# A hybrid encoder layer on one core: one softmax minimum for both key halves, and division by the sums after the value products

## The chip, the cores and the metric

One core of one Trainium2 chip. The metric is device time in microseconds, of one launch of the whole kernel. TensorE does the matrix products, VectorE and ScalarE read and empty PSUM, GpSimd works on SBUF only, and all transfers are issued by SyncE (SP).

## What is computed

The reference is one encoder layer, run on a prompt of 1024 tokens ("p") and a sample of 512 tokens ("s"). Each goes through one input projection, then two groups of heads side by side (a gated delta rule, 8 heads, and dense latent attention, 8 heads), gates, one output projection and a norm. The change touches only the dense attention:

```python
s = jnp.einsum('bhqd,bhkd->bhqk', qi, k) * MLA_SCALE
p = jax.nn.softmax(s, axis=-1)
return jnp.einsum('bhqk,bhkd->bhqd', p, v)
...
mix = jnp.concatenate([o_a * jax.nn.silu(z_a), o_b * jax.nn.silu(z_b)], axis=-1)
```

## The kernel before

Products are made in float32 by splitting an operand into a rounded high part and the rest, and adding three products. The program has stages: the input projection of p, that of s beside the delta rule of p, the preparation of the attention, the attention of p beside the delta rule of s, the attention of s beside the first output projection, and the rest of the output projection.

TensorE's order is written out by hand in all of them: `merge` keeps a clock `self.t`, advanced by `cost` for each product (line 116), and takes the next piece from the first stream whose due time has come; if none is due, the clock jumps. The clock fixes the order alone: TensorE then runs that order as fast as its operands come. The delta rule's streams stand first (so they win when due), the attention next, the output projection last (it fills). The other engines are ordered by the framework.

In `attention` (line 943) a head's queries go in blocks of 256, a block in two tiles of 128 queries, a tile against its keys in pieces of 512: two halves for p (nh = 2, 64 tiles), one for s (nh = 1, 32 tiles).

- `scores` (line 1007): for each half five products into one of two PSUM banks "s" (lines 1030 to 1034), their minimum on VectorE (`am`, 1037; the scores carry a minus sign), the exponential on ScalarE with that half's own minimum and the row sum beside it (`pe`, `al`, 1038). After the second half: the common minimum (1046), exp of the difference (`af`, ScalarE, 1047), the corrected sum (1048), its reciprocal (1049) and the two factors (1050), all on columns of 1 or 2 elements; then GpSimd multiplies both halves of `pe` by their factor (1052). For s there is a reciprocal (1043) and one such product.
- `values` (line 1076): one step takes 256 keys of a block: four transposes of `pe` into the one PSUM bank `pt` (1091), the split of it into `pth` (ScalarE, 196) and `ptl` (VectorE, 199), and, for the step before, six products with the values into `po` (`pv`, 1060). A block of p needs four steps, one of s two. After the last, VectorE multiplies `po` by the gate `z` (tile `az`, two buffers, 1073) and SP writes it to the scratch tensor `mix` (1074), which the output projection reads later.
- `beside` (line 1105) sets the rhythm: one half of scores, one step of values, and so on. A half is due SLAT = 3.0 after the half before the last one ended, a step PLAT = 2.0 after the last step ended. A block's transposes begin LAG = 2 halves after it was queued.

In `run`, `attentions` (line 1311) runs p, then s after a delay, and `first` (line 1289) begins the output projection once the delta rule is done; its weights are split on ScalarE and GpSimd (`whi`, `wlo`, `piece`, line 201).

Of the kernel before, what the change touches and what calls it, by code (L numbers as in the profile page):

```python
# [7 lines left out]
F32 = mybir.dt.float32  # L8
# [3 lines left out]
AF = mybir.ActivationFunctionType  # L12
ALU = mybir.AluOpType
AX = mybir.AxisListType
# [3 lines left out]
P = 128  # L18
D = 2048
KT = D // P  # L20
H = 8
# [4 lines left out]
BLK = 512  # L26
# [2 lines left out]
GAP = 8  # L29
PLAT = 2.0  # L30
SLAT = 3.0


QKV0, ZA0, CQ0, CKV0, ZB0, LAST = 0, 24, 32, 36, 38, 46
# [23 lines left out]
class Kern:  # L58
# [884 lines left out]
    def attention(self, q, T, cp, ap, pss, ps1):  # L943
        nc, a, sm, S = self.nc, self.a, self.sm, self.scratch
        nt, nh = T // P, T // BLK
        QB = 256
        def twice(out, src):
            nc.sync.dma_start(out[:64], src)
            nc.sync.dma_start(out[64:], src)
# [17 lines left out]
                    nc.vector.tensor_sub(krl[:64, ks], r[:64], krs[:64, ks].bitcast(F32))  # L967
        for h in range(H):
            self.dt(f"mix{8 + h}{q}", [P, T])

        bank = lambda name: pss.tile([P, BLK], F32, tag="s", name=name, bufs=2)

# [34 lines left out]
        def scores(h, kh, kl, t0, pes):  # L1007
            tq = slice(t0, t0 + QB)
            qn = ap.tile([P, QB], F32, tag="qn", name="qn")
            qp = ap.tile([P, QB], F32, tag="qp", name="qp")  # L1010
            nc.sync.dma_start(qn, S[f"q{h}{q}"][:, tq])
            twice(qp, S[f"qr{h // 2}{q}"][h % 2 * 64:h % 2 * 64 + 64, tq])
            qh = ap.tile([P, QB], F32R, tag="qh", name="qh", bufs=2)
            ql = ap.tile([P, QB], F32R, tag="ql", name="ql", bufs=2)
            self.split(qh, ql, qn)

            qr = ap.tile([P, QB], F32R, tag="qr", name="qr", bufs=2)
            nc.scalar.activation(qr, qp, AF.Copy)
            nc.vector.tensor_sub(qr[64:], qp[64:], qr[64:].bitcast(F32))
            for i in range(QB // P):  # L1020
                qs = slice(i * P, (i + 1) * P)
                pe = []
                m = sm.tile([P, nh], F32, tag="am", name="am", bufs=4)
                l = sm.tile([P, nh], F32, tag="al", name="al", bufs=4)
                f = sm.tile([P, nh], F32, tag="af", name="af", bufs=4)
                for k in range(nh):
                    ks = slice(k * BLK, (k + 1) * BLK)
                    pe.append(ap.tile([P, BLK], F32, tag="pe", name="pe", bufs=8 if nh > 1 else 6))
                    o = bank("s")
                    nc.tensor.matmul(o, qh[:, qs], kh[:, ks], start=True, stop=False)  # L1030
                    nc.tensor.matmul(o, qh[:, qs], kl[:, ks], start=False, stop=False)
                    nc.tensor.matmul(o, ql[:, qs], kh[:, ks], start=False, stop=False)
                    nc.tensor.matmul(o, qr[:, qs], krs[:, ks], start=False, stop=False)
                    nc.tensor.matmul(o, qr[:, qs], krl[:, ks], start=False, stop=True)
                    self.cost(BLK, 5)

                    nc.vector.tensor_reduce(m[:, k:k + 1], o, axis=AX.X, op=ALU.min)  # L1037
                    nc.scalar.activation(pe[k], o, AF.Exp, bias=m[:, k:k + 1], scale=-1.0,  # L1038
                                         accum_out=l[:, k:k + 1])
                    if k == nh - 1:  # L1040
                        mm = sm.tile([P, 1], F32, tag="amm", name="amm", bufs=4)
                        if nh == 1:
                            nc.vector.reciprocal(f, l)
                        else:

                            nc.vector.tensor_tensor(mm, m[:, 0:1], m[:, 1:2], op=ALU.min)
                            nc.scalar.activation(f, m, AF.Exp, bias=mm, scale=-1.0)
                            nc.vector.scalar_tensor_tensor(l, l, 1.0, f, op0=ALU.mult, op1=ALU.mult, accum_out=mm)
                            nc.vector.reciprocal(mm, mm)
                            nc.vector.tensor_scalar(f, f, mm, None, op0=ALU.mult)  # L1050
                        for k2 in range(nh):
                            nc.gpsimd.tensor_mul(pe[k2], pe[k2], f[:, k2:k2 + 1].to_broadcast([P, BLK]))  # L1052
                    yield
                pes.append(pe)


        past, done, tick = [0.0, 0.0], [0.0], [0]
        queue, now, last = [], [None], [None]

        def pv(b, kb, hi, lo):  # L1060
            vh, vl = b["vs"]
            if kb == 0:
                b["po"] = ps1.tile([P, QB], F32, tag="po", name="po")
                b["z"] = ap.tile([P, QB], F32, tag="az", name="az", bufs=2)
                nc.sync.dma_start(b["z"], S[f"f{ZB0 + b['h']}{q}"][:, b["tq"]])
            po, z = b["po"], b["z"]
            for j in range(2):
                nc.tensor.matmul(po, vh[:, kb + j], hi[:, j], start=kb + j == 0, stop=False)
                nc.tensor.matmul(po, vh[:, kb + j], lo[:, j], start=False, stop=False)
                nc.tensor.matmul(po, vl[:, kb + j], hi[:, j], start=False, stop=kb + j == nt - 1)  # L1070
            self.cost(2 * QB, 3)
            if kb + 2 == nt:
                nc.vector.tensor_mul(z, po, z)
                nc.sync.dma_start(S[f"mix{8 + b['h']}{q}"][:, b["tq"]], z)

        def values():

            if now[0] is None and queue and queue[0]["tick"] <= tick[0]:
                now[0] = queue.pop(0)
                now[0]["kb"] = 0  # L1080
            b, new = now[0], None
            if b is None and last[0] is None:
                return
            yield max(self.t, done[0] + PLAT)
            if b is not None:
                kb = b["kb"]
                pt = ps1.tile([P, 2, QB], F32, tag="pt", name="pt")
                for j in range(2):
                    k, c = (kb + j) // 4, (kb + j) % 4 * P
                    for i in range(QB // P):  # L1090
                        nc.tensor.transpose(pt[:, j, i * P:(i + 1) * P], b["pes"][i][k][:, c:c + P], self.ident)  # L1091
                self.cost(2 * QB, 2)
                hi = ap.tile([P, 2, QB], F32R, tag="pth", name="pth", bufs=2)
                lo = ap.tile([P, 2, QB], F32R, tag="ptl", name="ptl", bufs=2)
                self.split(hi, lo, pt)
                new = b, kb, hi, lo
                b["kb"] += 2
                if b["kb"] == nt:
                    now[0] = None
            if last[0] is not None:  # L1100
                pv(*last[0])
            last[0] = new
            done[0] = self.t

        def beside(gen):
            while True:
                yield max(self.t, past[0] + SLAT)
                try:
                    next(gen)
                except StopIteration as e:  # L1110
                    return e.value
                past[:] = past[1], self.t
                tick[0] += 1
                yield from values()

        def finish():
            while queue or now[0] is not None or last[0] is not None:
                tick[0] += 1
                yield from values()

        vs = []
        for h in range(H):
            if h % 2 == 0:
                wk = self.piece(a["w_uk"][h // 2], nc.gpsimd, ap, "2", 2, rb=3 - nh)
            kh, kl = yield from beside(keys(h % 2, wk))
            for t0 in range(0, T, QB):
                pes = []
                yield from beside(scores(h, kh, kl, t0, pes))
                if h % 2 == 0 and t0 == 0:
                    yield from finish()  # L1130
                    wv = self.piece(a["w_uv"][h // 2], nc.gpsimd, ap, "2", 2, rb=3 - nh)
                    yield from beside(pair_values(wv, vs))
                queue.append({"h": h, "tq": slice(t0, t0 + QB), "pes": pes, "tick": tick[0] + LAG,
                              "vs": [v[:, :, h % 2 * P:(h % 2 + 1) * P] for v in vs]})
        yield from finish()


# [273 lines left out]
```

## Time and profile before

| | |
|---|---|
| median of 3 runs | 3258.99 us (3256.91 to 3262.88) |
| the profiled execution's own time | 3260.19 us |
| its span in the trace | 3258.2 us |
| busy: TensorE, VectorE, ScalarE, GpSimd | 96%, 51%, 36%, 28% |
| scores of p and s on TensorE | 2081.6 to 2760.0 us of the span |

The profiled execution is taken on its own time, which is 1.2 us above the median. Times in the rows are microseconds from the start of the span. A matmul's record lasts from its start to its modelled end, so that records overlap: what a product costs TensorE is the distance from its start to the next start.

### The profile page before, as it was taken

What the parts mean: (1) busy time and instruction counts of PE and PEld (TensorE: products, weight loads), DVE (VectorE), ACT (ScalarE), POOL (GpSimd) and SP (SyncE); (2) the same over time, 40 slices, a digit from 0 to 9 for tenths busy, and PEclk for the clock granted to TensorE, in tenths of its full rate; (3) what the DMA queues carried; (4) which work ended last, traced back from release to release, by engine and by line L of the source; (5) the groups of instructions that cost most, each with busy time, mean ns of one, the idle gap of its engine ahead of it and who ended that gap; (6) DMA issues with size and microseconds to landing.
All of it is one profiled execution on the core that took longest, in us unless ns stands there. A gap on an engine that the chain in (4) does not pass through costs nothing.

```text
span 3258.2 us, 47587 instructions
## 1 busy us (share of the span) xinstructions
PE 3137.4 (96%) x16554; PEld 2617.6 (80%) x16554; DVE 1655.6 (51%) x4000; ACT 1173.7 (36%) x2768; POOL 904.4 (28%) x838
## 2 busy tenths in 40 slices
PE   7999999999999899999999999899999999999998
PEld 6888888888888788888888777688787878777876
DVE  7233343444411636764675488788887555240213
ACT  4222222222211323333333243466666555432231
POOL 5322222222222300000000034222233444464452
PEclk9999999999999999999999999999999999999999
DMA  7555555555555765655655775432223242563554
GB/s 244 172 164 171 168 167 172 174 172 162 172 181 155 265 197 183 189 190 185 226 172 176 226 253 173 132 95 85 62 79 109 69 138 81 168 197 122 151 171 132
DMA packets 352624, 529.57 MB, mean 163 GB/s; under 512 B 84656, under 2 KB 135848, under 8 KB 350848
## 3 DMA queue, kind: packets, MB, share of 16 engines
q1 hardware_dynamic: 352384, 526.54, 51.6%
q8 instruction: 130, 2.13, 0.3%
q14 instruction: 110, 0.90, 0.1%
HBM read 336.01 MB, written 186.86 MB: 160 GB/s over the span
## 4 chain that ended last, share of the span: by engine, by line
PE 74%; DVE 10%; DMA 8%; issue 3%; ACT 2%; POOL 2%; SPq 1%; POOLq 0%; DVEq 0%; ACTq 0%
PE mm L241 15%; PE mm L245 15%; PE mm L242 15%; DMA wraw<-w_out 3%; PE py L1169 3%; PE py L1168 3%; PE py L1170 3%; PE pt L1091 2%; PE Tp L808 2%; POOL wlo L199 2%; DVE UA L703 1%; PE Fp L790 1%; PE py L871 1%; PE pu L890 1%; DVE tm L754 1%
## 5 line engine op out<-in xcount | busy, mean ns | idle before, releaser
L241 PE MATMUL mm<-hi,whi 128*128 128x512 f32 x2256 | 900.8, 402 | 13.8 <-DVE lo L272 7.3
L199 POOL TENSOR_TENSOR wlo<-wraw,whi 128x512 fp32r<-128x512 f32 x432 | 582.6, 1354 | 1091.7 <-ACT whi L196 926.3
L242 PE MATMUL mm<-lo,whi 128*128 128x512 f32 x2256 | 877.9, 391 | 6.6 <-DVE lo L272 6.6
L245 PE MATMUL mm<-hi,wlo 128*128 128x512 f32 x2256 | 763.8, 391 | 0.0
L196 ACT ACTIVATE whi<-wraw 128x512 fp32r<-128x512 f32 x432 | 270.1, 630 | 941.3 <-PE mm L242 597.0
L241 PEld LDWEIGHTS mm<-hi,whi 128*128 128x128 f32 x2256 | 425.9, 189 | 99.2 <-ACT whi L196 8.5
L242 PEld LDWEIGHTS mm<-lo,whi 128*128 128x128 f32 x2256 | 425.6, 189 | 91.1 <-DVE lo L272 9.4
L245 PEld LDWEIGHTS mm<-hi,wlo 128*128 128x128 f32 x2256 | 424.8, 188 | 91.2 <-DMA wlo<-wl43.4_7823 0.3
L1168 PE MATMUL py<-whi,mhi 128*128 128x512 f32 x768 | 303.5, 395 | 9.1 <-DVE y L1183 6.2
L1169 PE MATMUL py<-wlo,mhi 128*128 128x512 f32 x768 | 304.1, 396 | 6.8 <-POOL wlo L199 6.8
L1170 PE MATMUL py<-whi,mlo 128*128 128x512 f32 x768 | 302.6, 394 | 0.0
L1052 POOL TENSOR_TENSOR pe<-pe,af 128x512 f32<-128x512 f32 x160 | 166.3, 1057 | 372.5 <-DVE af L1050 197.4
L323 DVE SCALAR_TENSOR_TENSOR acc<-cin,conv_w,acc 128x1024 f32<-128x1024 f32 (+1 forms) x192 | 208.9, 1088 | 33.8 <-ACT acc L321 29.2
L319 DVE TENSOR_TENSOR cin<-mm,rbh 128x512 f32<-128x512 f32 x72 | 47.5, 688 | 318.8 <-PE mm L245 269.3
L1169 PEld LDWEIGHTS py<-wlo,mhi 128*128 128x128 f32 x768 | 145.0, 189 | 44.2 <-POOL wlo L199 12.8
L1168 PEld LDWEIGHTS py<-whi,mhi 128*128 128x128 f32 x768 | 145.0, 189 | 43.7 <-DVE y L1183 7.8
L1170 PEld LDWEIGHTS py<-whi,mlo 128*128 128x128 f32 x768 | 145.0, 189 | 32.1
L327 DVE TENSOR_TENSOR acc<-mm,rbh 128x512 f32<-128x512 f32 x48 | 31.7, 687 | 233.5 <-PE mm L245 233.3
L1183 DVE TENSOR_TENSOR y<-py,g 128x512 f32<-128x512 f32 x36 | 24.7, 690 | 240.3 <-ACT junk L1182 236.7
L1038 ACT ACTIVATE pe<-s,am 128x512 f32<-128x512 f32 x160 | 110.2, 689 | 89.4 <-DVE am L1037 79.0
L199 DVE TENSOR_TENSOR ptl<-pt,pth 128x512 fp32r<-128x512 f32 x160 | 110.0, 687 | 51.7 <-ACT pth L196 50.8
L329 ACT ACTIVATE ct<-acc 128x1024 f32<-128x1024 f32 (+1 forms) x80 | 68.2, 853 | 159.7 <-DVE acc L323 126.1
(449 smaller groups left out, 5106.6 us busy)
## 6 DMA issues: line engine op xcount, KB each, us to landing
wraw<-w_out SPq DMA_DIRECT2D x192, 256.0 KB
wraw<-w_in SPq DMA_DIRECT2D x188, 256.0 KB
dd<-dX SPq DMA_DIRECT2D x48, 256.0 KB
wraw<-w_uq SPq DMA_DIRECT2D x36, 256.0 KB
x<-xT_p SPq DMA_DIRECT2D x16, 512.0 KB
xres<-x_p SPq DMA_DIRECT2D x8, 1024.0 KB
y_p<-y SPq DMA_DIRECT2D x32, 256.0 KB
x<-xT_s SPq DMA_DIRECT2D x16, 256.0 KB
```

Of the source, the lines that this page charges most:

```text
L196: nc.scalar.activation(hi, src, AF.Copy)
L199: (lo_eng or nc.vector).tensor_sub(lo, src, hi.bitcast(F32))
L241: nc.tensor.matmul(ps, whi[:, k], hi[:, s], start=kt == 0, stop=False)
L242: nc.tensor.matmul(ps, whi[:, k], lo[:, s], start=False, stop=False)
L245: nc.tensor.matmul(ps, wlo[:, k], hi[:, s], start=False, stop=kt == KT - 1)
L323: nc.vector.scalar_tensor_tensor(acc, cin[:, j:j + T], w[:, f, j:j + 1], acc, op0=ALU.mult, op1=ALU.add)
L329: nc.scalar.activation(t, acc, AF.Tanh)
L1038: nc.scalar.activation(pe[k], o, AF.Exp, bias=m[:, k:k + 1], scale=-1.0, accum_out=l[:, k:k + 1])
L1052: nc.gpsimd.tensor_mul(pe[k2], pe[k2], f[:, k2:k2 + 1].to_broadcast([P, BLK]))
L1168: nc.tensor.matmul(ps, hi[:, c], w[0], start=kt == kts[0], stop=False)
L1169: nc.tensor.matmul(ps, hi[:, c], w[1], start=False, stop=False)
L1170: nc.tensor.matmul(ps, lo[:, c], w[0], start=False, stop=kt == kts[1] - 1)
```

## The change

Both halves of a tile are now scored back to back; both exponentials take the common minimum, so that no factor is needed for them; `pe` is left undivided. The row sums of a block are added and inverted once per block on VectorE, written to a scratch tensor by SP, read back spread over all partitions, and GpSimd divides the gated output of the block (128 by 256) with them. The write of the inverse sums is queued two halves later, that of `mix` two steps of values later. A tile's first half is due HLAT = 2.4 after the last half's end (p); its second half at once; two steps of values follow a tile of p. For s the rhythm stays: one half, one step.

```diff
+HLAT = 2.4
...
+        self.dt("rl" + q, [H, T])
...
+            l = sm.tile([P, QB // P, nh], F32, tag="al", name="al", bufs=3)
+            rl = sm.tile([P, QB // P], F32, tag="ar", name="ar", bufs=4)
             for i in range(QB // P):
...
                     nc.vector.tensor_reduce(m[:, k:k + 1], o, axis=AX.X, op=ALU.min)
-                    nc.scalar.activation(pe[k], o, AF.Exp, bias=m[:, k:k + 1], scale=-1.0,
-                                         accum_out=l[:, k:k + 1])
-                    if k == nh - 1:
-                        mm = sm.tile([P, 1], F32, tag="amm", name="amm", bufs=4)
-                        if nh == 1:
-                            nc.vector.reciprocal(f, l)
-                        else:
-
-                            nc.vector.tensor_tensor(mm, m[:, 0:1], m[:, 1:2], op=ALU.min)
-                            nc.scalar.activation(f, m, AF.Exp, bias=mm, scale=-1.0)
-                            nc.vector.scalar_tensor_tensor(l, l, 1.0, f, op0=ALU.mult, op1=ALU.mult, accum_out=mm)
-                            nc.vector.reciprocal(mm, mm)
-                            nc.vector.tensor_scalar(f, f, mm, None, op0=ALU.mult)
-                        for k2 in range(nh):
-                            nc.gpsimd.tensor_mul(pe[k2], pe[k2], f[:, k2:k2 + 1].to_broadcast([P, BLK]))
-                    yield
+                    if k < nh - 1:
+                        yield True
+                mm = m
+                if nh > 1:
+                    mm = sm.tile([P, 1], F32, tag="amm", name="amm", bufs=4)
+                    nc.vector.tensor_tensor(mm, m[:, 0:1], m[:, 1:2], op=ALU.min)
+                for k, o in enumerate(os):
+                    nc.scalar.activation(pe[k], o, AF.Exp, bias=mm, scale=-1.0, accum_out=l[:, i, k:k + 1])
                 pes.append(pe)
+                if i == QB // P - 1:
+
+                    src = l[:, :, 0]
+                    if nh > 1:
+                        nc.vector.tensor_reduce(rl, l, axis=AX.X, op=ALU.add)
+                        src = rl
+                    nc.vector.reciprocal(rl, src)
+                    sums.append((tick[0] + 2, h, tq, rl))
+                yield
...
                 nc.vector.tensor_mul(z, po, z)
-                nc.sync.dma_start(S[f"mix{8 + b['h']}{q}"][:, b["tq"]], z)
+                rb = cp.tile([P, BLK], F32, tag="raw", name="rlb")[:, :QB]
+                nc.sync.dma_start(rb, S["rl" + q][b["h"]:b["h"] + 1, b["tq"]].to_broadcast([P, QB]))
+                nc.gpsimd.tensor_mul(z, z, rb)
+                outs.append((step[0] + 2, S[f"mix{8 + b['h']}{q}"][:, b["tq"]], z))
...
+            step[0] += 1
+            while outs and outs[0][0] <= step[0]:
+                nc.sync.dma_start(*outs.pop(0)[1:])
+            while sums and sums[0][0] <= tick[0]:
+                _, h, tq, rl = sums.pop(0)
+                nc.sync.dma_start(S["rl" + q][h:h + 1, tq].rearrange("a (i p) -> p (a i)", p=P), rl)
...
         def beside(gen):
+            part = 0
             while True:
-                yield max(self.t, past[0] + SLAT)
+
+                yield self.t if part else max(self.t, past[1] + HLAT if nh > 1 else past[0] + SLAT)
                 try:
-                    next(gen)
+                    half = next(gen)
                 except StopIteration as e:
                     return e.value
                 past[:] = past[1], self.t
                 tick[0] += 1
+                part = part + 1 if half else 0
+                if part:
+                    continue
                 yield from values()
+                if nh > 1:
+                    yield from values()
...
-            while queue or now[0] is not None or last[0] is not None:
+            while queue or now[0] is not None or last[0] is not None or outs:
```

## Rows read from the trace of the kernel before

**Rows 1.** The page, section 1: busy time of each engine, share of the span

```profile
PE 3137.4 (96%) x16554; PEld 2617.6 (80%) x16554; DVE 1655.6 (51%) x4000; ACT 1173.7 (36%) x2768; POOL 904.4 (28%) x838
```

**Rows 2.** Busy time by stretch: PE, PEld, DVE, ACT, POOL, PEclk, DMA share, GB/s

```profile
2200.00:2300.00 100.00, 94.92 (x702) 84.02 (x701) 83.33 (x259) 61.20 (x179) 27.17 (x28) 1.00 0.29 85
...
2400.00:2500.00 100.00, 98.00 (x703) 87.64 (x702) 76.31 (x220) 61.63 (x180) 30.24 (x29) 1.00 0.21 65
2500.00:2590.00 90.00, 84.12 (x481) 71.41 (x480) 59.38 (x146) 51.94 (x124) 39.39 (x36) 0.98 0.33 108
```

**Rows 3.** Waits of TensorE, 2060 to 2610 us: total us, times, longest

```profile
PE pt L1091 <- DVE ptl L199: 10.7, 12, 1.8
PE pt L1091 <- DVE amm L1046: 3.2, 2, 1.7
PE pt L1091 <- POOL pe L1052: 2.4, 4, 1.0
...
PE s L1030 <- ACT pe L1038: 2.2, 2, 1.2
PE pt L1091 <- DVE al L1048: 2.1, 2, 1.8
```

**Rows 4.** Timelines of TensorE, VectorE and GpSimd around one such wait

```profile
2291.21 0.60 PE L1091 MATMUL pt<-ident,pe 128*128 128x128 f32 x4
...
2295.81 0.63 PE L1091 MATMUL pt<-ident,pe 128*128 128x128 f32 x4 [1.69 <-DVE amm L1046]
...
2294.98 0.68 DVE L199 TENSOR_TENSOR ptl<-pt,pth 128x512 fp32r<-128x512 f32 x1
2295.58 0.15 DVE L1046 TENSOR_TENSOR amm<-am 128x1 f32<-128x1 f32 x1
...
2296.94 2.04 POOL L1052 TENSOR_TENSOR pe<-pe,af 128x512 f32<-128x512 f32 x2 [7.67 <-DVE af L1050]
```

**Rows 5.** Timeline, 2426 to 2429 us, where only attention runs on TensorE

```profile
2426.68 0.60 PE L1091 MATMUL pt<-ident,pe 128*128 128x128 f32 x4
...
2427.32 0.60 ACT L196 ACTIVATE pth<-pt 128x512 fp32r<-128x512 f32 x1 [1.72 <-PE pt L1091]
...
2427.83 0.39 PE L1030 MATMUL s<-kh,qh 128*128 128x512 f32 x1
2427.95 0.69 DVE L199 TENSOR_TENSOR ptl<-pt,pth 128x512 fp32r<-128x512 f32 x1 [0.37 <-ACT pth L196]
...
2428.99 0.60 PE L1091 MATMUL pt<-ident,pe 128*128 128x128 f32 x4
```

**Rows 6.** Groups of instructions: busy us, mean ns of one, idle before

```profile
L1052 POOL TENSOR_TENSOR pe<-pe,af 128x512 f32<-128x512 f32 x160 | 166.3, 1057 | 372.5 <-DVE af L1050 197.4 <-DVE af L1043 50.2 <-PE pt L1091 22.5
...
L1047 ACT ACTIVATE af<-am,amm 128x2 f32<-128x2 f32 x64 | 19.2, 300 | 4.8 <-DVE amm L1046 4.2
...
L1050 DVE TENSOR_SCALAR af<-af,amm 128x2 f32<-128x2 f32 x64 | 15.4, 241 | 2.9
...
L1048 DVE SCALAR_TENSOR_TENSOR al<-al,af 128x2 f32<-128x2 f32 x64 | 11.1, 173 | 4.5 <-ACT af L1047 4.0
L1049 DVE RECIPROCAL amm<-amm 128x1 f32<-128x1 f32 x64 | 10.2, 159 | 0.8
```

**Rows 7.** Timeline of TensorE: two pieces of the delta rule between attention's

```profile
2263.94 1.05 PE L849 MATMUL pk<-st,KQ 128*128 128x128 f32 x8
2264.83 1.06 PE L852 MATMUL pk<-st,KQ 128*128 128x128 f32 x8
2265.73 0.60 PE L1091 MATMUL pt<-ident,pe 128*128 128x128 f32 x4
```

**Rows 8.** A load's issue on SP, and the ScalarE instruction that waits for it

```profile
2617.94 0.32 SPq L1011 DMA_DIRECT2D qn<-q0s  x1
...
2620.08 0.42 ACT L196 ACTIVATE qh<-qn 128x256 fp32r<-128x256 f32 x1 [1.62 <-DMA qn<-q0s]
```

**Rows 9.** The instructions of tile qn: duration ns min/median/max, first and last start

```profile
L199 DVE TENSOR_TENSOR ql<-qn,qh x48: 415/426/1499, 2070.7 to 2745.8; 128x256 fp32r<-128x256 f32 x48
```

More of the change, by code (lines that the diff above doesn't have):

```diff
@@ L1019, in scores @@
             nc.vector.tensor_sub(qr[64:], qp[64:], qr[64:].bitcast(F32))
+            l = sm.tile([P, QB // P, nh], F32, tag="al", name="al", bufs=3)
+            rl = sm.tile([P, QB // P], F32, tag="ar", name="ar", bufs=4)
             for i in range(QB // P):
                 qs = slice(i * P, (i + 1) * P)
-                pe = []
+                pe, os = [], []
                 m = sm.tile([P, nh], F32, tag="am", name="am", bufs=4)
-                l = sm.tile([P, nh], F32, tag="al", name="al", bufs=4)
-                f = sm.tile([P, nh], F32, tag="af", name="af", bufs=4)
                 for k in range(nh):
@@ L1035, in scores @@
                     self.cost(BLK, 5)
+                    os.append(o)
                     nc.vector.tensor_reduce(m[:, k:k + 1], o, axis=AX.X, op=ALU.min)
-                    nc.scalar.activation(pe[k], o, AF.Exp, bias=m[:, k:k + 1], scale=-1.0,
-                                         accum_out=l[:, k:k + 1])
-                    if k == nh - 1:
-                        mm = sm.tile([P, 1], F32, tag="amm", name="amm", bufs=4)
-                        if nh == 1:
-                            nc.vector.reciprocal(f, l)
-                        else:
-                            nc.vector.tensor_tensor(mm, m[:, 0:1], m[:, 1:2], op=ALU.min)
-                            nc.scalar.activation(f, m, AF.Exp, bias=mm, scale=-1.0)
-                            nc.vector.scalar_tensor_tensor(l, l, 1.0, f, op0=ALU.mult, op1=ALU.mult, accum_out=mm)
-                            nc.vector.reciprocal(mm, mm)
-                            nc.vector.tensor_scalar(f, f, mm, None, op0=ALU.mult)
-                        for k2 in range(nh):
-                            nc.gpsimd.tensor_mul(pe[k2], pe[k2], f[:, k2:k2 + 1].to_broadcast([P, BLK]))
-                    yield
-                pes.append(pe)
+                    if k < nh - 1:
[6 more added lines that the diff above has]
+                    nc.scalar.activation(pe[k], o, AF.Exp, bias=mm, scale=-1.0, accum_out=l[:, i, k:k + 1])
+                pes.append(pe)
+                if i == QB // P - 1:
[6 more added lines that the diff above has]
+                yield
         past, done, tick = [0.0, 0.0], [0.0], [0]
-        queue, now, last = [], [None], [None]
+        queue, now, last, sums, outs, step = [], [None], [None], [], [], [0]
         def pv(b, kb, hi, lo):
```

## The prediction

> **What bounds the kernel now.** The page's busy times come first: TensorE has work for 96% of the span [rows 1], and the change neither adds nor removes a matrix product. So only time in which TensorE stands still can be won or lost. The stretches show how little that is in the attention: 95 of 100 us and 98 of 100 us busy in two stretches of p's attention, 84 of 90 where the delta rule has ended [rows 2]. VectorE is the second busiest there, at 83 and 76 of 100 us.
>
> Then I ask what TensorE waits for, between the beginning of p's attention and its end [rows 3]. Five entries matter. One is the chain that the change is aimed at: the transposes wait for GpSimd's scaled `pe`, 2.4 us in 4 waits. Three are transposes waiting for VectorE: 10.7 us under `ptl`, 3.2 under `amm`, 2.1 under `al`. The last two names are misleading, and one place shows it: the transposes of 2295.81 us are put down to `amm`, but GpSimd scaled that tile only at 2296.94, after them, and the instruction just in front of `amm` is the `ptl` that began at 2294.98 and lasted 0.68 [rows 4]. They waited for their PSUM bank `pt`, which that `ptl` emptied; the step before had filled it at 2291.21. So I read 10.7 + 3.2 + 2.1 = 16.0 us as one wait, that for the bank `pt`. The fifth, 2.2 us, is a score waiting for a bank "s" that an exponential still reads.
>
> **The change, part by part.** The sum is made against the profiled execution's own 3260.2 us, which is 1.2 above the median.
>
> *Small work removed.* For each of p's 64 tiles ScalarE loses 0.300 us, VectorE 0.241 + 0.173 + 0.159 = 0.573 us [rows 6], 36.7 us in all. What comes back is a reduce and a reciprocal per block of two tiles on VectorE; with the reciprocal's 0.159 us for each it is 32 x 0.318 = 10.2 us. s trades 32 reciprocals for 16. None of this is on TensorE's path by itself: it shortens queues in which `pth` and `ptl` stand, which is counted with the bank `pt` below.
>
> *Scaling on GpSimd removed.* 160 instructions of 1.057 us, 166.3 us [rows 6], become 48 on half the columns, 25 us by half the duration. GpSimd is not the bound; what reaches TensorE is the wait of 2.4 us. **It goes: -2.4 us.** The new product stands behind the last product of a block, where no transpose waits for it.
>
> *The new rhythm.* For p a tile was half, step, half, step; it becomes half, half, step, step. Between the second step of a tile and the first of the next there are now two halves: the bank `pt` has always been emptied by then, and that part of the 16.0 us goes. Between the two steps of one tile there is no half any more, only what the delta rule or the output projection puts there. The shortest such interval can be read where attention runs alone [rows 5]: transposes at 2426.68, the next piece at 2427.83, so a step occupies TensorE for 1.15 us; the bank is free when `ptl` ends, 2427.95 + 0.69 = 2428.64, 1.96 us after the transposes began. Today a half fills the rest and the next transposes come at 2428.99, without a wait. Without that half TensorE would stand 1.96 - 1.15 = 0.81 us. With a piece of the delta rule in the hole it would not: the smallest common one takes 0.89 us (2263.94 to 2264.83), two of them 1.79 [rows 7], and 1.15 + 0.89 = 2.04 covers 1.96. So the cost is between 0 (every hole filled) and 64 x 0.81 = 51.8 us (none). The hand-written clock leaves 2.0 between the steps, time in which the delta rule's streams win and the output projection, last in rank, may enter too; so most holes will be filled. I take one in five unfilled, near the lower end because TensorE is 95% and more busy in these stretches with all streams together: **+10.4 us**. Of the old 16.0 us I take all away, **-16.0 us**, since this term now holds the whole wait for `pt`. Loaded queues stretch the chain (from 2291.21 to 2295.66 it took 4.45 us [rows 4]), and the lighter VectorE shortens it again; I let these cancel, and keep the ends.
>
> *The score banks.* Both banks are held until the common minimum is known. The first half of the next tile comes after two steps, at least 2 x 1.15 us and one chain later, about 3.1 us; it needs a full-width pass of VectorE (0.69 us, as `ptl`), the small minimum, and one of ScalarE (0.60 us, as `pth`) [rows 5], some 1.6 us with the hand-overs. Today's wait is 2.2 us [rows 3]; I leave it as it is. Ends: -2.2 if it vanishes, +64 x 0.2 = 13 us if loaded queues make each tile late by a fifth of a microsecond. The exponentials of a tile now follow each other on ScalarE; `pth` may queue behind one (0.60 us by the same row), which belongs to the same upper end.
>
> *The way through memory.* Per block SP issues one write of 256 single elements and one spread load, 96 more issues, by 0.32 us each [rows 8] 31 us of SP's queue over 700 us. A load is used 2.1 us after its issue (2617.94 to 2620.08 [rows 8]); the scattered write has no row, and I bound it by that and by twice that. The load comes four steps after the write for p, two for s, at over 2.3 us a step, so it need not wait. GpSimd then waits for the load; behind it stand `wlo` splits for the output projection, which are made ahead. SP's `mix` write waits for GpSimd, but is queued two steps later, some 4.6 us against 2.1 + 0.5. Only where `finish` empties the pipeline, before the values of each pair of heads, does that write come at once, with the load of the next value weights queued behind it on SP: 4 pairs for p and 4 for s at up to 2.7 us would be 21 us if nothing hid them; those weights are loaded ahead of need, so I take 0. The `z` tile is held two steps longer; with two buffers the next load still has a whole block's time. A gain there is excluded: the path has no wait today.
>
> *s's attention* keeps its rhythm, so I take 0 there.
>
> Sum: -2.4 - 16.0 + 10.4 = -8.0 us: 3252.2 on the profiled execution, **3251 us** on the median.
>
> One observation bears on how much VectorE gains. The split `ql` reads two SBUF tiles; of 48 its median is 426 ns and its longest 1499 [rows 9], though the work is the same. The Trainium skill, "GPSIMD Engine Reference", section 1 (Specifications), says that GpSimd shares its SBUF interfaces with VectorE and collides with VectorE instructions that have two SBUF inputs. The trace fits that, without showing it alone; by that rule the removal of 141 us of GpSimd work would shorten such instructions and nothing of the PSUM ones, and the sum would come out below mine, as in rival 3.
>
> **Rivals.**
>
> 1. *The paired steps stall.* Where: the second transposes of each p tile, on the bank `pt`. If two holes in three are unfilled or filled too briefly: 51.8 x 2/3 = 34.5, and 34.5 - 18.4 = +16.1 us, 3275 us on the median. It cancels the gain from 18.4/51.8 = 36% unfilled, and is slower by 0.2% from 48%. For it: the delta rule's pieces come about once in two attention pieces, and VectorE is 83% busy. Against it: two other groups of streams may enter the hole. Chance 0.25.
> 2. *One wait for another.* The pairs give back what the rest saves, about a third unfilled: 3258 us, within 6.5 us either way. For it: TensorE stands still for so little in these stretches. Chance 0.25.
> 3. *VectorE is relieved more than its own instructions show*, by less company from GpSimd, so that no hole waits: 3260.2 - 18.4 - 1.2 = 3241 us. For it: the 1499 ns. Against it: `ptl` and the minimum read PSUM, and a stretched instruction mostly costs nothing. Chance 0.08.
>
> **How the numbers follow.** My forecast, a gain of about 8 us, has 0.42. A measurement of this kernel can tell about 0.2%, 6.5 us, from no change. The forecast reaches from -18 to -2; I put 0.34 of its 0.42 beyond 6.5 us. Faster: 0.34 + 0.08 = 0.42. Same: 0.08 + 0.25 = 0.33. Slower: 0.25. The range goes down to rival 3 and a little further for the score banks' 2.2 us, 3238, and up to rival 1, 3274. The forecast's own range is 3241 to 3257.
>
> **What would show it.** Right: the same count of products; GpSimd's scaling gone; the wait of transposes for VectorE in p's attention below 16 us in total, with those that are left all at a tile's second step; the entry for GpSimd gone; VectorE's busy share there several per cent lower. Wrong: waits of 0.8 us at most second steps (rival 1); long waits of scores for ScalarE (the banks); TensorE or SP waiting for the inverse sums.

## The result, and the profile after

| | before | after |
|---|---|---|
| median | 3259.99 us (4 runs, 3256.91 to 3262.88) | 3399.99 us (4 runs, 3394.12 to 3408.64) |
| ratio | | 1.043, 95% interval 1.0417 to 1.0443 |
| span of the profiled execution | 3258.2 us | 3406.9 us |
| mean granted clock of TensorE | 0.990 | 0.970 |

The change makes the kernel 140 us slower. The forecast was 3251 us, its range ended at 3274: the time moved the other way and lies far outside the range. Up to 2060 us, before the attention of p, the two kernels have nearly the same busy times (TensorE 2007 and 2010 us); all of it arises behind that.

First the page's busy times, the row that answers to [rows 1]:

```profile
PE 3182.7 (93%) x16554; PEld 2657.4 (78%) x16554; DVE 1619.1 (48%) x3792; ACT 1160.7 (34%) x2704; POOL 776.9 (23%) x726
```

The same 16554 products. VectorE, ScalarE and GpSimd have less to do than before, so none of them became the bound by its own work. Then the stretches (columns as in [rows 2]; the first three are the same stretches as there):

```profile
2200.00:2300.00 100.00, 83.94 (x607) 75.87 (x608) 68.31 (x209) 52.67 (x150) 6.31 (x9) 0.93 0.31 76
2400.00:2500.00 100.00, 88.65 (x638) 79.17 (x637) 60.45 (x161) 51.97 (x149) 4.95 (x6) 0.97 0.20 51
2500.00:2590.00 90.00, 61.68 (x318) 52.27 (x318) 39.13 (x76) 35.06 (x77) 13.54 (x13) 0.83 0.45 118
2600.00:2700.00 100.00, 98.12 (x572) 83.68 (x571) 50.99 (x105) 49.51 (x112) 18.05 (x17) 1.00 0.40 65
2800.00:2900.00 100.00, 72.47 (x379) 60.77 (x378) 38.11 (x72) 35.80 (x82) 19.18 (x18) 0.86 0.50 75
```

TensorE works 84 of 100 us where it was 95, and 62 of 90 where it was 84. The granted clock, the number before the DMA share, is 0.83 to 0.97 where it was 0.98 to 1.00. In the stretch at 2600 us, where the output projection fills, nothing is lost. What TensorE waits for, 2060 to 2800 us (p's attention now ends near 2700):

```profile
PE pt L1104 <- DVE ptl L200: 64.6, 33, 12.4
PE Dp L780 <- DMA dd<-dX: 9.7, 3, 5.3
...
PE s L1032 <- ACT pe L1048: 4.4, 4, 1.9
```

The entry for GpSimd's scaling is gone. The wait for the bank `pt`, 16.0 us in all before [rows 3], is four times that, and one of them lasts 12.4 us, which no queue of 0.7 us instructions makes. So I looked at that one, in the timelines of SP, VectorE and TensorE:

```profile
2502.10 0.43 SPq L1090 DMA_DIRECT2D rlp<-ar  x1
2503.84 0.32 SPq L930 DMA_DIRECT2D z<-f31s  x1
2504.26 0.38 SPq L1087 DMA_DIRECT2D mix12p<-az  x1
2515.07 0.32 SPq L940 DMA_DIRECT2D mix7s<-z  x1
...
2514.29 0.75 DVE L937 SCALAR_TENSOR_TENSOR z<-oT,norm_g,z 128x512 f32<-128x512 f32 x1 [11.68 <-DMA z<-f31s]
...
2515.55 0.68 DVE L200 TENSOR_TENSOR ptl<-pt,pth 128x512 fp32r<-128x512 f32 x1
...
2516.29 1.11 PE L1104 MATMUL pt<-ident,pe 128*128 128x128 f32 x4 [12.39 <-DVE ptl L200]
```

Read from the bottom: TensorE stands 12.39 us for the bank; the `ptl` that empties it begins at 2515.55; VectorE, in order, had stood 11.68 us at a gate of the delta rule for the load of `z`; that load was issued at 2503.84, 1.74 us after a write of inverse sums (`rlp<-ar`), and was used 10.45 us after its issue. The bank is only where a late transfer becomes visible. SP stands too, in the whole run:

```profile
SPq L1079 <- DMA rlp<-ar: 105.0, 22, 7.8
...
SPq L1079 <- DMA rls<-ar: 48.7, 12, 7.2
```

L1079 is the spread load, waiting for the write of its own block. The load has nothing else to wait for, so SP arrives at it directly behind the write: the first write was issued at 2103.29, its load at 2111.53, 8.24 us later. Over p's 32 blocks this distance has a median of 8.8 us and is never under 7.4.

The slow clock adds to this. Inside the wait of 12.39 us and just after it (columns as above):

```profile
2508.00:2509.00 1.00, 0.00 (x0) 0.00 (x0) 0.00 (x0) 0.00 (x0) 0.00 (x0) 0.96 0.52 48
2509.00:2510.00 1.00, 0.00 (x0) 0.00 (x0) 0.00 (x0) 0.00 (x0) 0.00 (x0) 0.50 0.42 46
...
2517.00:2518.00 1.00, 1.00 (x6) 1.00 (x5) 0.00 (x0) 0.56 (x1) 0.00 (x0) 0.50 0.98 106
```

TensorE stands, the granted clock falls to 0.50, the lower level of 1.2 GHz, and in the microsecond from 2517, when TensorE is busy throughout again, it is still 0.50. Over the profiled executions (1 - 0.970) x 3406.9 = 102 us of full clock were not granted, against 33 before.

The listed waits of TensorE from 2060 to 3000 us, every entry added up, rose from 53.0 to 150.4 us: +97. With +70 of clock that is 167 where 149 were lost; the two overlap, since a wait in a slow stretch counts in both. The page divides the 149 without overlap: TensorE had nothing to do for 103 us more, and it was busy for 45 us more with the same number of products.

### The profile page after: what moved, and what is told of

Read it like the earlier page. It is cut to its first block, busy times and chain, and to the rows that moved or that the text cites. A ratio compares the mean times of both kernels' runs of the same rounds, so it can differ in the third digit from the quotient of the medians.

```text
span 3406.9 us, 47123 instructions
## 1 busy us (share of the span) xinstructions
PE 3182.7 (93%) x16554; PEld 2657.4 (78%) x16554; DVE 1619.1 (48%) x3792; ACT 1160.7 (34%) x2704; POOL 776.9 (23%) x726
## 4 chain that ended last, share of the span: by engine, by line
PE 71%; DMA 12%; DVE 8%; issue 3%; ACT 3%; SPq 2%; POOL 2%; DVEq 0%; ACTq 0%; POOLq 0%
PE mm L242 14%; PE mm L246 14%; PE mm L243 14%; DMA wraw<-w_out 3%; PE py L1188 3%; PE py L1190 3%; PE py L1189 3%; PE Tp L809 2%; POOL wlo L200 2%; PE pt L1104 1%; DMA rlp<-ar 1%; PE Fp L791 1%; PE pu L891 1%; PE py L872 1%; PE pu L888 1%
## 5 line engine op out<-in xcount | busy, mean ns | idle before, releaser
L1104 PE MATMUL pt<-ident,pe 128*128 128x128 f32 x640 | 104.4, 288 | 90.8 <-DVE ptl L200 90.4
L1104 PEld LDWEIGHTS pt<-ident,pe 128*128 128x128 f32 x640 | 80.1, 147 | 115.0 <-DVE ptl L200 91.6
L1040 DVE TENSOR_REDUCE am<-s 128x1 f32<-128x512 f32 x160 | 109.8, 687 | 73.9 <-PE s L1036 73.6
```

## The experiments

Theory A at first: the single-element write lands late and SP, in order, stands behind it; the rhythm costs nothing. The first four kernels take the change apart.

**The route without its transfers, the rhythm alone, the route alone, the sums as rows.**

```diff
# e1_no_route, against the changed kernel: GpSimd multiplies by ones
-                nc.sync.dma_start(rb, S["rl" + q][...].to_broadcast([P, QB]))
-                nc.gpsimd.tensor_mul(z, z, rb)
+                nc.gpsimd.tensor_mul(z, z, one)
...
-                nc.sync.dma_start(S["rl" + q][h:h + 1, tq].rearrange("a (i p) -> p (a i)", p=P), rl)
# e2_rhythm_alone, against the changed kernel: each tile's pe scaled on GpSimd by its own inverse sum, mix written at once
...
+                for k2 in range(nh):
+                    nc.gpsimd.tensor_mul(pe[k2], pe[k2], f.to_broadcast([P, BLK]))
...
# e3_route_alone, against the kernel before: write, spread load, product and later mix; the sums are ones
...
+                            nc.vector.tensor_scalar(rl, m[:, 0:1].to_broadcast([P, QB // P]), 0.0, 1.0, op0=ALU.mult, op1=ALU.add)
...
# e4_rows, against the changed kernel: sums turned on VectorE, two writes of 4 rows of 128 bytes
...
+                    nc.vector.transpose(rt, rl)
...
+                for i in range(QB // P):
+                    nc.sync.dma_start(S["rl" + q][h:h + 1, tq].rearrange("a (i b c) -> (a i) b c", b=P // 32, c=32)[i], rl[i::32])
```

> The changed kernel without the way through memory: the inverse sums are neither written nor loaded, and GpSimd multiplies the output of a block by a tile of ones (so the division by the sums is left out). Rhythm, GpSimd product and late queueing of mix stay. Theory A (SP stands behind the load of the inverse sums, which waits some 8 us for the write of single elements; later loads come late): 3245 to 3265 us. Rival B (the paired rhythm makes TensorE wait): 3360 us or more. Rival C (the long hold of z and the late mix write): 3300 us or more.

> Paired rhythm and common minimum, but GpSimd divides both halves of each tile by its sum before the transposes, as in the kernel before, and mix is written at once: no way through memory, no late queueing. Theory A: 3245 to 3265 us, no more than 10 from the run without the way through memory. Rival B: 3360 us or more.

> The kernel before with its own rhythm and scaling, and the way through memory beside it, carrying ones: one write of 256 single elements, one spread load and one GpSimd product per block, mix queued two steps later. Theory A: 3360 us or more, with SP waiting for the write some 150 us in total. Rival B: 3260 to 3280 us.

> The changed kernel, with the inverse sums turned by a VectorE transpose of 32 by 32 blocks first, so that the write goes out as 2 transfers of 4 rows of 128 bytes in place of 256 single elements. Theory A with the single elements as the cause of the 8 us: the write lands in 2 to 3 us, SP waits under 60 us for it, and the kernel takes 3250 to 3300 us. If any write followed by its load costs the same: 3380 us or more.

Measured, beside 3257.05 of the kernel before: e1 3301.09 (1.0127, 1.0108 to 1.0145); e2 3317.20 (1.0180, 1.0157 to 1.0204); e3 3377.4 in a single run; e4 3306.99 (1.0147, 1.0128 to 1.0167). So the route costs 99 us in the new rhythm (3399.99 - 3301.09) and 120 in the old one, and 93 of the 99 hang on how the sums are written: as eight rows in place of 256 single elements they are nearly free. That part of theory A held; that the rhythm costs nothing fell: without the route it costs 44 to 60 us, between the prices of theories A and B of e1 and e2. The time of e1 is that of its rival C, the long hold of `z` and the late write of `mix`; but e2 has neither and is no faster, so they are not needed for this loss. One forecast of e3 failed too: SP waited 64 us for the writes at its spread loads (23.0 for p, 40.5 for s), not some 150, and the route cost 120 all the same.

The `z` load of above in e4, on SP and VectorE, with the writes of rows ahead of it:

```profile
2470.37 1.07 SPq L1094 DMA_DIRECT2D rlp<-art  x2
2471.56 0.36 SPq L930 DMA_DIRECT2D z<-f31s  x1
...
2474.31 0.75 DVE L937 SCALAR_TENSOR_TENSOR z<-oT,norm_g,z 128x512 f32<-128x512 f32 x1 [1.04 <-DMA z<-f31s]
```

2.75 us from issue to use, in place of 10.45.

**Who waits for the write: SP's order, its queue, or every transfer?**

```diff
# e5_pool_queue, against the changed kernel (load and mix on GpSimd, the write stays on SP)
-                nc.sync.dma_start(rb, S["rl" + q][...].to_broadcast([P, QB]))
+                nc.gpsimd.dma_start(rb, S["rl" + q][...].to_broadcast([P, QB]))
...
-                nc.sync.dma_start(*outs.pop(0)[1:])
+                nc.gpsimd.dma_start(*outs.pop(0)[1:])
# e8_write_away (only the write on GpSimd); e9_all_away makes this replacement and those of e5
-                nc.sync.dma_start(S["rl" + q][h:h + 1, tq].rearrange("a (i p) -> p (a i)", p=P), rl)
+                nc.gpsimd.dma_start(S["rl" + q][h:h + 1, tq].rearrange("a (i p) -> p (a i)", p=P), rl)
# e11_unread, against e4_rows: one more write, to a tensor that nobody reads
+                nc.sync.dma_start(S["rd" + q][h:h + 1, tq].rearrange("a (i p) -> p (a i)", p=P), rl[:, :2])
```

> The changed kernel with its single-element write still on SP, but with the spread load and the write of mix issued by GpSimd. Theory A (SP, which works in order, stands some 8 us behind each such write at the load that reads it back, and the loads of q, z and the delta rule behind it come late): SP is free, GpSimd stands in its place, and little on GpSimd is urgent here: 3300 to 3330 us, near the 3307 of the kernel that writes rows, and TensorE's waits for pt fall from 64.6 to about 32 us. Rival B (the 256 small packets slow all other transfers by themselves, whoever waits for them): 3370 us or more, as in the changed kernel. Rival C (GpSimd's standing still delays splits and memsets that TensorE needs): 3330 to 3380 us, with waits on POOL in TensorE's list.

> The changed kernel with the single-element write issued by GpSimd, through GpSimd's own queue; the spread load and the write of mix stay on SP, and SP still has to stand at the load until that write has landed. Theory B (the write blocks the queue it goes through: a load issued behind it on the same queue lands some 8 us late): other loads are no longer behind it in the queue, only behind SP's standing still, and the time is between 3307 and the changed kernel's 3400 us; the more of the 93 us comes from SP standing still, the nearer to 3400. Theory B alone: 3310 to 3345 us. Rival A (SP standing still is enough to make the loads late): 3370 to 3400 us. Rival D (the small packets slow all 16 DMA engines, whatever the queue): 3380 us or more, here and in the next kernel.

> The changed kernel with all three transfers of the route on GpSimd: the single-element write, the spread load, the write of mix. Theory B (the write blocks its own queue) and rival A (SP stands still) both give 3300 to 3330 us, since neither SP nor its queue has anything to do with the write. Rival D (the small packets slow the DMA engines for everybody): 3370 us or more. With the kernel that leaves only the write on SP at 3394 us, a time near 3310 here says that the write's place in SP's queue is the cause.

> The kernel that writes the sums as rows, with one more write per block in front of them: the 256 inverse sums as single elements to a scratch tensor that nobody reads. SP waits for nothing more than before. Theory B (the write blocks the queue for what is issued behind it): 3370 to 3410 us, with loads issued behind it 8 us and more late (the load of z that is used 2.7 us after its issue without the write, 10.5 with it). Rival A (only SP's standing still at the load that reads it back costs): 3305 to 3320 us.

Measured: e5 3394.32 (1.0413, 1.0395 to 1.0430), e8 3416.15 (1.0475, 1.0458 to 1.0492), e9 3408.46 (1.0457, 1.0440 to 1.0474), e11 3420.32 (1.0491, 1.0469 to 1.0514). Theory A fell with e5, and its rival B was met: SP no longer stands at the load, and nothing is won. GpSimd now stands there in its place; rival C of e5, which expected 3330 to 3380 us from that, is not met by the time. The `z` load shows why (SP and VectorE of e5):

```profile
2499.44 0.43 SPq L1090 DMA_DIRECT2D rlp<-ar  x1
2501.17 0.32 SPq L930 DMA_DIRECT2D z<-f31s  x1
...
2511.65 0.75 DVE L937 SCALAR_TENSOR_TENSOR z<-oT,norm_g,z 128x512 f32<-128x512 f32 x1 [12.00 <-DMA z<-f31s]
```

10.5 us again, though SP stands at no load of the sums any more. In the stretches of e5 the transfers that start behind the write are seen to crawl (the last two columns: DMA share of 16 engines, counted where a packet starts, and GB/s):

```profile
2501.00:2502.00 1.00, 0.00 (x0) 0.00 (x0) 0.00 (x0) 0.91 (x2) 0.35 (x1) 1.00 0.11 41
2502.00:2503.00 1.00, 0.00 (x0) 0.00 (x0) 0.00 (x0) 0.00 (x0) 0.00 (x0) 1.00 3.46 139
2503.00:2504.00 1.00, 0.00 (x0) 0.00 (x0) 0.00 (x0) 0.00 (x0) 0.00 (x0) 1.00 0.00 0
2504.00:2505.00 1.00, 0.00 (x0) 0.00 (x0) 0.00 (x0) 0.00 (x0) 0.00 (x0) 1.00 0.48 37
```

The packets that start between 2502 and 2503 need 3.46 x 16 = 55 us of engine time; after them 37 GB/s move, and TensorE, VectorE and ScalarE all stand.

e8 and e9 were to split what rival B had left together: whether only the write's own queue is blocked (theory B there) or all of them (rival D). Theory B fell: with all three transfers on GpSimd's queue and none of the route on SP, the time stays at 3408. SP's loads are late all the same (waits of e9, 2060 to 3000 us):

```profile
DVE z L937 <- DMA z<-f31s: 12.2, 1, 12.2
ACT qh L197 <- DMA qn<-q6s: 12.1, 1, 12.1
...
PE Dp L780 <- DMA dd<-dX: 10.8, 3, 6.9
```

The write itself, now issued by GpSimd, has its landing on record (e9's list of transfers; the last number is the median from issue to landing):

```profile
rlp<-ar POOLq DMA_DIRECT2D x32, 1.0 KB, 9.2
```

So the write slows transfers in the other queue too, as rival D had it; e8, at 3416, lies above the 3370 to 3400 that rival A gave it. e11 agrees: one unread write per block brings 113 us back. My remark there that SP would wait for nothing more was wrong, since the writes of rows behind the unread one land late as well, and SP stood 105 us at p's spread loads; but e9 shows the loss without that.

The records of the single packets say the same for whole runs. From 2060 to 3000 us, packets that took more than 4 us: 46 in the changed kernel, 52 in e3, 46 in e5, 39 in e8, 43 in e9, 53 in e11; none in the kernel before, e1, e2 and e4. Most are packets of 2 KB, as in the loads of `z`; the median of such a packet in the changed kernel is 84 ns. The packets of 4 bytes have a median of 9 ns there: the time is not in their own records, but in those of larger packets.

**Number of small writes, or the place where they land?**

```diff
# e12_spaced, against e11_unread: the same 256 elements, 512 bytes apart
-        self.dt("rd" + q, [H, T])
+        self.dt("rd" + q, [H, T, P])
...
-                nc.sync.dma_start(S["rd" + q][h:h + 1, tq].rearrange("a (i p) -> p (a i)", p=P), rl[:, :2])
+                nc.sync.dma_start(S["rd" + q][h:h + 1, tq, 0:1].rearrange("a (i p) o -> p (a i o)", p=P), rl[:, :2])
```

> As the kernel with the unread write, but the 256 elements go to places 512 bytes apart in the scratch tensor, in place of next to each other. Theory E (256 small writes into the same 1 KB of memory wait for each other there, and all other transfers behind them): the extra write costs little, 3305 to 3330 us. Rival F (each write of 4 bytes costs by itself, wherever it goes): 3390 us or more, as with the neighbouring elements (3420).

Measured: 3305.63 (1.0134, 1.0120 to 1.0148), the time of e4 without any such write: theory E held. The same 256 elements of 4 bytes, in the same queue at the same place of the order, cost 113 us next to each other and nothing that can be measured 512 bytes apart; the packets under 512 bytes are as many (99248 in e11, 99249 here), and none from 2060 to 3000 us takes over 4 us. The `z` load behind one:

```profile
2467.15 0.38 SPq L1094 DMA_DIRECT2D rdp<-art  x1
2468.29 0.32 SPq L930 DMA_DIRECT2D z<-f31s  x1
...
2471.00 0.75 DVE L937 SCALAR_TENSOR_TENSOR z<-oT,norm_g,z 128x512 f32<-128x512 f32 x1 [0.94 <-PE kp L986]
```

It is there in at most 2.7 us; VectorE waits for something else. So it is not the number of packets, nor their size alone: what counts is where they go, into the same 1 KB or apart. That they wait for each other in the one place is a reading of this, not seen in any record; seen is what is held up behind them. The Trainium skill, "DMA: Bandwidth & Descriptors", Specifications, says that transfers below 512 bytes are done by reading, changing and writing back. That could make neighbours in one piece of memory wait for each other, which no run here shows; by itself it does not say that such writes cost nothing when they are apart, as e12 shows. How near two of them must be to collide was not tried, and e12 spreads the elements over 128 KB, so that distance and spread were not told apart.

**Where the other 44 to 60 us come from.**

```diff
# e6_old_order, against e4_rows: common minimum, but half, step, half, step
-                yield self.t if part else max(self.t, past[1] + HLAT if nh > 1 else past[0] + SLAT)
+                yield max(self.t, past[1] + HLAT if nh > 1 and not part else past[0] + SLAT)
...
-                if part:
-                    continue
                 yield from values()
-                if nh > 1:
-                    yield from values()
# e7_wide_hole, against e4_rows: the second step of a pair due 3.2 after the first
...
-                    yield from values()
+                    yield from values(3.2)
# e13_pairs_own_min, against the kernel before: only the order of the changed kernel
-                    yield
+                    yield k < nh - 1
...
+                if part:
+                    continue
                 yield from values()
+                if nh > 1:
+                    yield from values()
# e10_sample_only, against the kernel before: p untouched, s divides later, sums as rows
...
-                        for k2 in range(nh):
+                        for k2 in range(nh if nh > 1 else 0):
...
```

> The kernel that writes the sums as rows, with the common minimum kept but the order of before: half, step, half, step; only the first half of a tile keeps its due time of 2.4. Theory A (the cost of 44 us or more comes from the two steps in a row, whose second one waits for pt): the waits for pt fall to 16 us or less, the held score banks cost up to 13 us, and the time is 3250 to 3275 us. Rival B (it comes from holding both score banks until the common minimum is known): first halves of tiles wait for the exponential at most tiles, 0.5 to 1 us each, 32 to 64 us in all, and the time is 3290 to 3330 us.

> The kernel that writes the sums as rows, with the paired steps kept, but for p the second step of a pair due 3.2 after the first in place of 2.0, so that other streams have longer to come in between. Theory A (second steps wait because too little stands between them): pieces move into the hole, the waits for pt fall from 32 to below 20 us, and the time is 3285 to 3300 us. Rival B (where the hole is empty no other stream has a piece that is due, and elsewhere the pieces only change places): same as the 3307 us without it, within 5 us, with the waits for pt between 28 and 35 us.

> The kernel of before with its arithmetic unchanged (each half with its own minimum, factors and scaling of the probabilities on GpSimd, no way through memory), only the order on TensorE is the changed one: half, half, step, step for p. Theory A (the two steps in a row are enough for the loss of 40 to 60 us, since the second one waits for pt): 3295 to 3320 us, with waits for pt near 32 us in all. Rival G (the pairs alone cost little, and the loss needs the common minimum, which lengthens the way from the scores to the transposes and holds both score banks): 3250 to 3275 us.

> The kernel of before for p; only s's attention has its sums divided after the value products, with the sums written as rows. Theory A (the loss that is left when the route is repaired comes from the common minimum of p's two halves, and s, which has one half, gains little or nothing by the later division): within 8 us of before, 3252 to 3268 us, with TensorE's waits up to 2600 us as before. Rival (the later division costs by itself, as more transfers on SP while the output projection loads its weights): 3270 to 3290 us.

Each ratio is taken against runs of the kernel before that were made beside that kernel.

| kernel | order | minimum | median us | ratio (95%) | waits for `pt`, 2060 to 2660 us |
|---|---|---|---|---|---|
| before | old | own | 3259.99 | | 20.4 |
| e13 | pairs | own | 3325.42 | 1.0184 (1.0167 to 1.0201) | 50.3 |
| e4 | pairs | common | 3306.99 | 1.0147 (1.0128 to 1.0167) | 32.6 |
| e7 | pairs, wider hole | common | 3310.84 | 1.0151 (1.0134 to 1.0169) | 17.6 |
| e6 | old | common | 3310.14 | 1.0156 (1.0141 to 1.0172) | 5.7 |
| e10 | old | own | 3255.96 | 0.9992 (0.9983 to 1.0000) | 19.7 |

The three rows of e13's 50.3 us (waits of TensorE):

```profile
PE pt L1092 <- DVE ptl L200: 39.4, 33, 4.4
PE pt L1092 <- POOL pe L1053: 8.2, 4, 3.1
...
PE pt L1092 <- DVE al L1049: 2.7, 2, 1.5
```

So the pairs alone, with the arithmetic of before, cost 62 us: theory A of e13 held, and its numbers were too low (3320 at most, with 32 us of these waits). In the old order the common minimum, with the sums as rows and first halves due at 2.4, costs 50 (waits of e6):

```profile
PE s L1033 <- ACT pe L1049: 37.0, 32, 2.4
PE kp L983 <- ACT pe L1049: 7.8, 4, 3.7
...
PE vp L1001 <- ACT pe L1049: 2.8, 4, 1.6
```

These are the score banks, which `kp` and `vp` use too, held by the exponentials: 47.6 us from 2060 to 2660, where it was 7.9 (the 2.2 of [rows 3], and 5.7 under `vp`, most of it behind the window of those rows); rival B of e6 held. The two costs do not add up. Each edit disturbs the rhythm in its own way, and together the pairs give the exponentials the time that the common minimum takes (10.3 us of such waits in the changed kernel) and pay with the hole between the two steps. Widening that hole halves the waits for `pt` (e7), as its theory A said, and no time is won, as its rival B said; neither held whole. Others grow in their place, as in these rows of e7 (4.4, 0 and 0.6 us in e4):

```profile
PE s L1033 <- ACT pe L1049: 7.2, 7, 2.2
...
PE py L872 <- ACT oacc L865: 5.0, 4, 1.5
PE py L872 <- DVE oacc L862: 4.2, 6, 0.8
```

Added up over all entries, 2060 to 3000 us, TensorE waits 81.8 us in e4, 82.6 in e7 and 86.4 in e6, against 53.0 before, for times within 4 us of each other. e10 shows that s's part of the change, with the sums as rows, is worth nothing that can be told from no change, and it is the best of all kernels tried; no version beat the kernel before by more than that.

## Why the prediction was wrong

**The way through memory, taken at 0, cost 93 to 99 us: the step that failed.** Three of its parts failed. *The scattered write has no row, and I bound it by 2.1 us and twice that*: it took 8.2. The lower row was that of a load with long rows, and nothing in the trace resembled 256 elements into one kilobyte; an upper bound of twice an unlike row was no bound. *The load comes four steps after the write, so it need not wait*: four steps of TensorE's order, but SP does not keep step with TensorE. It was at the load as soon as the write was issued, and stood there for 105 us over p: the prediction's own sign of being wrong, SP waiting for the inverse sums. *The upper end was 21 us, for loads behind a late `mix` write*: I looked only for what stands behind a waiting instruction, and not for what the transfer itself does to the transfers around it. That was the cost: e5, e8 and e9 moved SP's wait, its queue and the write's queue, and the time stayed; e12 took the neighbourhood away, and the cost went. The issues themselves, 31 us of SP by [rows 8], are hidden as predicted, but for the 6 us by which e4 is above e1.

**The bank `pt`: the mechanism was right, its size was not.** The 16.0 us did go: of the 30 waits for `pt` in e1, one, of 0.3 us, stands at a step with a half before it. And the share of empty holes was nearly right: in e1 11 of the 64 pairs have nothing of another stream between their steps (a few records of transposes are missing), one in six where I took one in five. But all 11 wait, 1.8 us each, 19.8 in all, not 0.81; and 18 of the filled ones wait as well, 11.6 us. The term measured 31.8 us, not 10.4. What failed is the 1.96 us, *the shortest such interval*, and with it *1.15 + 0.89 = 2.04 covers 1.96*. Between the start of a step's transposes and the end of their `ptl` lay in the kernel before a median of 2.9 us (2060 to 2420), 2.5 (2420 to 2520) and 2.4 (2520 to 2620), worked out from the records; 1.96 is the shortest of all. I took the one undisturbed chain for the usual one, though [rows 4] showed 4.45. Waits of TensorE in e1, to 2660 us, then one empty hole there (TensorE, ScalarE, VectorE):

```profile
PE pt L1105 <- DVE ptl L200: 31.8, 30, 3.3
...
PE s L1035 <- ACT pe L1051: 4.7, 5, 1.9
```

```profile
2460.01 0.60 PE L1105 MATMUL pt<-ident,pe 128*128 128x128 f32 x4
2462.71 0.63 PE L1105 MATMUL pt<-ident,pe 128*128 128x128 f32 x4 [1.40 <-DVE ptl L200]
...
2458.91 2.45 ACT L921 ACTIVATE oacc<-oacc,goy 128x128 f32<-128x128 f32 x8 [1.09 <-DVE goy L179]
2461.27 0.57 ACT L197 ACTIVATE pth<-pt 128x512 fp32r<-128x512 f32 x1
...
2461.87 0.69 DVE L200 TENSOR_TENSOR ptl<-pt,pth 128x512 fp32r<-128x512 f32 x1
```

The delta rule's eight activations hold ScalarE up to 2461.27, so `pth` begins 1.26 us after the transposes in place of 0.64 [rows 5], and the bank is free at 2462.56, 2.55 us after they began. Other streams help the hole on TensorE and lengthen the chain on ScalarE and VectorE. The bank is not the whole of the second loss either: to 3000 us its waits rose by 11 us (22.0 to 32.9) of the 28 in the next paragraph; the largest others, which had no place in the sum, are products waiting for `yb` (0 to 4.8) and for the split `kh` (0.7 to 5.3).

**The clock was left out of the sum.** In e1 the listed waits are 81.2 us against 53.0, +28, and (1 - 0.984) x 3301.0 = 53 us of full clock are missing against 33, +20. The page divides the 43 us by which the span grew: TensorE had nothing to do for 28 more and was busy for 14 more (3151.8 against 3137.4) with the same 16554 products. That the lower clock is what made them longer was not shown by itself; its 20 us are an upper end, since it costs nothing while TensorE waits.

The other steps held. The reading of the bound held. GpSimd's wait of 2.4 us is gone. The reduce and the reciprocal of a block take 155 and 164 ns, as taken. GpSimd's product is dearer than half of the old one, at no cost:

```profile
L1080 POOL TENSOR_TENSOR az<-az,rlb 128x256 f32<-128x256 f32 x48 | 35.8, 746 | 459.8 <-DVE az L1077 258.8 <-DVE amm L1046 82.8 <-issue 28.0
```

35.8 us, not 25, since 746 ns is 71% of 1057 for half the columns; the second operand is a whole tile now, where it was one column. The score banks' waits rose by 2.7 us with the pairs (7.9 to 10.6 in e1, `s` and `vp`), within the ends given. s's part was worth 0, as e10 shows. Of the rivals the first had the mechanism of the second loss and the right sign; by e1 its price was 44, not 16. The relief of rival 3 can be seen and was small: the splits `ql` of over 450 ns fell from 22 of 48 to 11, and all 48 together from 31.0 to 23.4 us. None of the rivals had the first and larger loss, which is why the range was too narrow; its upper end, 3274, did not even hold rival 1's own 3275.

## What to carry to other kernels

A write of single elements into neighbouring places of memory is not a small transfer: here it held up what was behind it, in both queues tried, for some 8 us each time. So turn such a column into rows on chip before it is written, or space the elements, as was tried with 512 bytes. When a transfer has no likeness in the trace, its upper end is not a multiple of the nearest row, and the question is also what it does to the transfers around it. The slack of a chain is read from its median among all the work that shares its engines, not from the one place where it runs alone.

## What the runs showed of the hardware that I had not expected

- 256 elements of 4 bytes next to each other: 8.2 us until SP could issue the load that waits for the first such write (never under 7.4 in p), 9.2 us from issue to landing where GpSimd issued them; and 10.5 us until a 256 KB load issued 1.7 us behind one was used, against 2.75 behind rows; 113 us over 48 such writes. 512 bytes apart: nothing measurable.
- The packets of 4 bytes last 9 ns in the records (median); it is larger packets that last over 4 us, 46 of them in the changed kernel and none in e12.
- The delay does not keep to the queue that the write goes through: the time was 3394 and 3400 us for writes issued by SP (e5 and the changed kernel), 3408 and 3416 for writes issued by GpSimd (e9 and e8).
- A wait of TensorE is paid more than once: the product that ended the wait of 12.39 us took 1.11 us in place of 0.60, and the stretch from 2500 to 2590 had a granted clock of 0.83, where it was 0.98 before.
